# A two-layer fp32 encoder on one core: TensorE's order taken from the program text, attention steps spread over three pump steps, and a lane of their own for the gates

## The chip, the cores and the metric

The kernel runs on one core of a Trainium2 chip. The metric is device time in microseconds (us), from one launch to its end; lower is better. The engines are TensorE (PE in the profile; its weight loads are listed apart as PEld), VectorE (DVE), ScalarE (ACT), GpSimd (POOL) and SyncE (SP, which issues most DMAs). A profiled execution also gives the span from its first to its last instruction.

## What is computed

Two layers of a bidirectional encoder on x of 256 tokens by 2048, all in fp32. Cut to what matters:

```python
for l in range(2):
    h = rms_norm(x, gpre_mix)
    p = h @ W_in                       # 2048 x 4624: attention q,k,v; mLSTM q,k,v,o; 16 gate columns
    A = window_attention(rope(q), rope(k), v, sink)      # 8 heads of 128, 2 KV heads
    M = mlstm(forward + backward, chunks of 128)         # 4 heads, qk 128, v 256
    x = x + rms_norm(concat(A, M) @ W_out, gpost_mix)    # 2048 x 2048
    u = relu(rms_norm(x, gpre_mlp) @ W_up) ** 2          # 2048 x 8192
    x = x + rms_norm(u @ W_down, gpost_mlp)              # 8192 x 2048
```

Nothing fits a single reduced-precision product, so every weight and every activation is split into a rounded part and a remainder, and each product is made of three matmuls.

## The kernel before, in words

**Tiles.** Tokens are two tiles of 128, called t = 0 and 1; a contraction of 2048 is 16 chunks of 128, called k. Each weight tile covers 512 output columns (in the input projection, tile 3 has 272 and tile 9 has 256). Per layer there are 10 "in" tiles, 4 "out" tiles, and four blocks b of 4 "up" and 4 "down" tiles.

**Weights.** `load` (L168) brings one weight tile in four pieces: a DMA into `raw` (two buffers), an ACT copy that rounds it to `whi` (L191), a DVE subtraction that leaves `wlo` (L192), both with four buffers. The first two pieces of the program come in four parts each.

**Products.** `mm_k` (L196) issues, for one k and one t, three matmuls of 512 columns: hi by hi (L203), hi by lo (L204), lo by hi (L205). An up tile other than the first of its layer goes through `mm_stationary` (L259) instead: there the weights stay in the array and 256 tokens stream, in two pairs, each of 2 x 16 x 3 matmuls of 256 columns (L272 to L274). One two-bank tile `mms` holds both pairs. After each pair `up_evac` (L846) runs a Relu on ACT (L848), a square, and a split.

**Activations.** `pre` (L327) makes four chunks of a transposed, scaled input: four PE transposes into `ptx` (L332), a DVE multiplication into `xg` (L336), and `split_T` (L323), which is an ACT copy (L324) and a subtraction (L325) on DVE or POOL. At the start of the program, stage q of tile 0 (four k's) first calls `pre` for t = 0, does its 12 matmuls for t = 0, then the same for t = 1. The first up tile of a layer ends in `up_first` (L837): Relu, Square, four transposes `ptu` (L843), a split, for each t.

**Side work.** Attention and mLSTM are written as generators that stand in two lists, `urgent` and `later`; `mm_tile` (L220) advances the first generator of a list by one step after each k, through `pump` (L210). `attend` (L369) yields after the scores of each token tile, three times (`SLACK`, L366) before its transposes, and once between the transposes `pp` (L411) and the products `po` (L417). `gates` (L425), a chain of scans, is called by `side_gates` from the list `urgent`.

**What sets the order.** All instructions stand in program text in one order, the order of emission. A scheduler then gives every engine its own order, by a timeline that it computes: an instruction may be moved ahead of others of its engine whose inputs it takes to come later. Before the change it does so for all engines. Once given, an engine's order is fixed: an engine works through its own list.

Of the kernel before, what the change touches and what calls it, by code (L numbers as in the profile page):

```python
# [86 lines left out]
def encoder_kernel(ctx, tc, x, wall, rope, conv_w, gate_bias, ml_g, sink, gpre, gpost, out):  # L87
# [117 lines left out]
        nc.tensor.matmul(dst, lhsT=xl, rhs=hi, start=False, stop=(k == KC - 1))  # L205


    urgent, later = [], []

    def pump():  # L210
        for lane in (urgent, later):
            while lane:
                try:
                    next(lane[0])
                    break
                except StopIteration:
                    lane.pop(0)
        return urgent or later

    def mm_tile(key, T, stages=(), after=None, at=None, half=False):  # L220

# [101 lines left out]
    def split_T(ps, hi, lo, eng=None):  # L323
        nc.scalar.activation(hi, ps, AF.Copy)  # L324
        (eng or nc.vector).tensor_tensor(out=lo, in0=ps, in1=hi.bitcast(F32), op=ALU.subtract)  # L325
# [40 lines left out]
    SLACK = 3  # L366
    ASC = float(HD) ** -0.5

    def attend(pair, qT, kT, vA, nsink, snk, attT):  # L369

        g = pair // 2
        q0 = 2 * (pair % 2)
        ptile = []
        for t in range(NT):
            sc = psax.tile([P, 2, SEQ], F32, tag="ax", name="sc")
            far = slice((1 - t) * P, (2 - t) * P)
            for j in range(2):
                nc.tensor.matmul(  # L378
                    sc[:, j], lhsT=qT[:, q0 + j, t * P:(t + 1) * P], rhs=kT[:, g], start=(j == 0), stop=False)

            nc.tensor.matmul(
                sc[:, :, far], lhsT=identr, rhs=dmask[:, 1 - t:2 - t].to_broadcast([P, 2, P]),
                start=False, stop=True)
            mx = small.tile([P, 2], F32, tag="mx", name="mx")
            nc.vector.tensor_reduce(out=mx, in_=sc, op=ALU.max, axis=AX.X)
            nm = small.tile([P, 2], F32, tag="nm", name="nm")
            nc.vector.scalar_tensor_tensor(
                out=nm, in0=mx, scalar=-ASC, in1=nsink[:, 2 * pair:2 * pair + 2], op0=ALU.mult, op1=ALU.min)
            es = small.tile([P, 2], F32, tag="es", name="es")
            nc.vector.tensor_tensor(out=es, in0=snk[:, 2 * pair:2 * pair + 2], in1=nm, op=ALU.add)  # L390
            nc.scalar.activation(es, es, AF.Exp)
            pr = f2k.tile([P, 2, SEQ], F32, tag="f2k", name="pr")
            rs = small.tile([P, 2], F32, tag="rs", name="rs")
            for j in range(2):
                nc.scalar.activation(
                    pr[:, j], sc[:, j], AF.Exp, bias=nm[:, j:j + 1], scale=ASC, accum_out=rs[:, j:j + 1])
            nc.vector.tensor_tensor(out=rs, in0=rs, in1=es, op=ALU.add)
            nc.vector.reciprocal(out=rs, in_=rs)
            for j in range(2):
                nc.vector.tensor_scalar(  # L400
                    out=pr[:, j], in0=pr[:, j], scalar1=rs[:, j:j + 1], scalar2=None, op0=ALU.mult)
            ptile.append(pr)
            yield
        for _ in range(SLACK):
            yield
        po = psax.tile([P, 2, SEQ], F32, tag="ax", name="po")
        for j in range(2):
            pp = psax.tile([P, 2, SEQ], F32, tag="ax", name="pp")
            for kb in range(2):
                for t in range(NT):  # L410
                    nc.tensor.transpose(  # L411
                        pp[:, kb, t * P:(t + 1) * P], ptile[t][:, j, kb * P:(kb + 1) * P], ident)
            pT = f2k.tile([P, 2, SEQ], F32, tag="f2k", name="pT")
            nc.scalar.activation(pT, pp, AF.Copy)
            yield
            for kb in range(2):
                nc.tensor.matmul(  # L417
                    po[:, j], lhsT=vA[:, kb, g * HD:(g + 1) * HD], rhs=pT[:, kb], start=(kb == 0), stop=(kb == 1))
        split_T(po, attT[:, 2 * pair:2 * pair + 2, 0, :], attT[:, 2 * pair:2 * pair + 2, 1, :])
# [2 lines left out]
    CF = 0.25 * float(HD) ** -0.5  # L422
    DIRS = ((0, 0, 1), (32, 1, 0))

    def gates(gp, cols):  # L425


        f = gp.rearrange("p c (d q h) -> p c d q h", d=2, q=2)
# [19 lines left out]
        for d in range(2):  # L448
# [2 lines left out]
            nc.vector.scalar_tensor_tensor(  # L451
                out=gpad[:, :, 1, c0:c0 + MH], in0=ac[:, :, d], scalar=-2.0, in1=z[:, :, d],
                op0=ALU.mult, op1=ALU.add)
        yield
        pr = psax.tile([P, 2, SEQ], F32, tag="ax", name="prow")
        for q in range(2):
            for c in range(NT):
# [38 lines left out]
        for r, r2 in ((rnm, rnm2), (rwi, rwi2)):  # L496
            nc.scalar.activation(r2[:NG], r, AF.Copy)
            nc.vector.tensor_tensor(out=r2[NG2:NG2 + NG], in0=r, in1=r2[:NG].bitcast(F32), op=ALU.subtract)
        yield
        yield  # L500
        yield
        pc = psax.tile([P, 6, NG], F32, tag="ax", name="pcol")
        for i, r in enumerate((re_, rwe, rb)):
            for c in range(NT):
                nc.tensor.transpose(pc[:, 2 * i + c], r[:, c * P:(c + 1) * P], ident[:NG, :NG])
        nc.vector.tensor_copy(cols, pc)

    def conv_silu(zp, cw, dst):

        y = f1k.tile([P, SEQ], F32, tag="f1k", name="cy")  # L510
        nc.scalar.activation(y, zp, AF.Copy, scale=cw[:, 1:2])
        nc.vector.scalar_tensor_tensor(
            out=y[:, 1:], in0=zp[:, :SEQ - 1], scalar=cw[:, 0:1], in1=y[:, 1:], op0=ALU.mult, op1=ALU.add)
        nc.vector.scalar_tensor_tensor(
            out=y[:, :SEQ - 1], in0=zp[:, 1:], scalar=cw[:, 2:3], in1=y[:, :SEQ - 1], op0=ALU.mult, op1=ALU.add)
        th = f1k.tile([P, SEQ], F32, tag="f1k", name="cth")
        nc.scalar.activation(th, y, AF.Tanh, scale=0.5)
        nc.vector.scalar_tensor_tensor(out=dst, in0=th, scalar=1.0, in1=y, op0=ALU.add, op1=ALU.mult)

    def qk_heads(ps, c0, heads, s, cw, qk):  # L520

        w = 2 * HD * len(heads)
        nat = []
        for t in range(NT):
            a = f2k.tile([P, 512], F32, tag="f2k", name="qkn")
            nc.scalar.activation(a[:, :w], ps[t][:, c0:c0 + w], AF.Copy, scale=s[t])
            nat.append(a)
            yield
        yield
        for i, h in enumerate(heads):  # L530
            pt = psax.tile([P, 2, SEQ], F32, tag="ax", name="ptqk")
            for j in range(2):
                for t in range(NT):
                    o = (2 * i + j) * HD
                    nc.tensor.transpose(pt[:, j, t * P:(t + 1) * P], nat[t][:, o:o + HD], ident)
            for j in range(2):
                conv_silu(pt[:, j], cw[:, j * MH + h], qk[:, h, j])
            yield

    def mlstm_head(h, qk, va, cols, hm, hr, name):  # L540


        st = psax.tile([P, SEQ], F32, tag="ax", name="st")
        for c in range(NT):
# [118 lines left out]
    for l in range(DEPTH):  # L663
        big = apool.tile([P, 4112], F32, tag="A", name="A_mix")
        va = big[:, :NT * MH * (DV + 1)].rearrange("p (c h e) -> p c h e", c=NT, h=MH)
        qk = big[:, 2064:4112].rearrange("p (h j t) -> p h j t", h=MH, j=2)
        hm = big[:, 2064:4112].rearrange("p (h c e) -> p h c e", h=MH, c=NT)
# [7 lines left out]
        sh = [lay.tile([P, 1], F32, tag=f"sh{t}", name="sh") for t in range(NT)]  # L675
        cols = lay.tile([P, 6, NG], F32, tag="cols", name="cols", bufs=1)
        hr = [None] * MH

        def scales():
            for t in range(NT):  # L680
                s1[t] = pre_scale(t, "s1")
                nc.vector.tensor_scalar(out=sh[t], in0=s1[t], scalar1=0.5, scalar2=None, op0=ALU.mult)
# [29 lines left out]
        def side_gates(ps):  # L712
            gp = small.tile([P, NT, 16], F32, tag="gp", name="gp", bufs=1)
            for t in range(NT):
                nc.vector.scalar_tensor_tensor(
                    out=gp[:, t], in0=ps[t][:, :16], scalar=s1[t], in1=gbias, op0=ALU.mult, op1=ALU.add)
            yield from qk_heads(ps, 16, [0], s1, cw, qk)
            yield from gates(gp, cols)

        def side_v(ps, c0, h0, nh):  # L720
            for t in range(NT):
                nc.scalar.activation(
                    va[:, t, h0:h0 + nh, :DV], ps[t][:, c0:c0 + nh * DV].rearrange("p (h e) -> p h e", h=nh),
                    AF.Copy, scale=s1[t])
            for h in range(h0, h0 + nh):
                later.append(mlstm_head(h, qk, va, cols, hm, hr, f"l{l}h{h}"))
            yield

        gated = []
# [25 lines left out]
        for grp in range(2):  # L755
            ps = in_tile(1 + grp)
            urgent.append(side_q(ps, grp))
        ps = in_tile(3)
        urgent.append(side_gates(ps))
        ps = in_tile(4)  # L760
        urgent.append(qk_heads(ps, 0, [1, 2], s1, cw, qk))
        ps = in_tile(5)
        urgent.append(qk_heads(ps, 0, [3], s1, cw, qk))
        urgent.append(side_v(ps, 256, 0, 1))
        g = [gload(2 * l, n) for n in range(3)]
        ps = in_tile(6)
# [192 lines left out]
```

## Time and profile before

| | |
|---|---|
| median of 3 runs | 2148.2 us (2144.47 to 2152.57) |
| the profiled execution | 2145.2 us |
| its span | 2143.4 us |
| PE busy | 2100.0 us, 98% of the span |
| DVE, ACT, POOL busy | 53%, 46%, 3% |
| mean granted clock of PE | 0.996 |
| DMA | 388.37 MB, mean 181 GB/s |
| the chain that ended last | PE 92%, DVE 2%, DMA 2%, ACT 2% |

A row of a timeline gives the start, the duration of one piece of work and, in brackets, the idle time of its engine just before it with what ended that. Matmuls overlap in the engine, so the listed duration of one (0.39 us for 512 columns) is longer than the distance between two starts (0.23 us); costs are therefore read from starts. A busy share of PE near one says little by itself for the same reason. The granted clock is 1.00 at the full 2.4 GHz and 0.5 at 1.2 GHz.

### The profile page before, as it was taken

To read this page: it belongs to the slowest core of one execution; us is meant where nothing else is said; L and a number is where in the kernel's file an instruction comes from. 1 tells how busy PE (TensorE), PEld (TensorE's weight loads), DVE (VectorE), ACT (ScalarE), POOL (GpSimd) and SP (SyncE) were. 2 spreads that over 40 slices of the span, in tenths; PEclk is the share of its full clock that TensorE was granted. 3 is DMA by queue.
4 is the path that set the end of the run, shared out by engine and by line. 5 is a ranking of instruction groups with operands and counts; after the bars stand their busy time and mean duration, and the time that the engine had idled before them with its cause. 6 is when DMAs were issued, how large, how long until landed. Compare 5 with 4: busy or idle time off the path is not lost.

```text
span 2143.4 us, 28980 instructions
## 1 busy us (share of the span) xinstructions
PE 2100.0 (98%) x12412; PEld 1855.3 (87%) x12412; DVE 1135.4 (53%) x1219; ACT 983.9 (46%) x1077; POOL 60.8 (3%) x68
## 2 busy tenths in 40 slices
PE   8999999999999999999999999999999999999998
PEld 6878887988998998898878788879889989989986
DVE  6656566544444444445567656464444444444454
ACT  5455545453443353345354555455445434533542
POOL 0000002000000000000020000030000000000000
PEclk9999999999999999999999999999999999999999
DMA  7434355555555455546444344545555555554553
GB/s 256 163 135 175 120 194 180 197 192 190 188 194 191 169 197 207 186 174 215 174 181 161 134 150 148 206 149 195 207 190 193 189 190 183 195 193 173 191 205 118
DMA packets 62209, 388.37 MB, mean 181 GB/s; under 512 B 9600, under 2 KB 10112, under 8 KB 17280
## 3 DMA queue, kind: packets, MB, share of 16 engines
q1 hardware_dynamic: 61936, 386.48, 51.4%
q8 instruction: 97, 1.59, 0.3%
q14 instruction: 32, 0.26, 0.0%
q10 hardware_dynamic: 144, 0.03, 0.0%
HBM read 384.39 MB, written 2.10 MB: 180 GB/s over the span
## 4 chain that ended last, share of the span: by engine, by line
PE 92%; DVE 2%; DMA 2%; ACT 2%; POOL 1%; issue 1%; SPq 1%; POOLq 0%; DVEq 0%; ACTq 0%
PE mm L205 19%; PE mm L204 19%; PE mm L203 19%; PE mms L272 10%; PE mms L274 10%; PE mms L273 10%; DMA raw<-wall 1%; PE sc L378 1%; PE pn L594 1%; DVE xs L792 1%; PE po L417 1%; DVE wlo L192 1%; POOL h2T L325 1%; ACT whi L191 0%; ACT uz L848 0%
## 5 line engine op out<-in xcount | busy, mean ns | idle before, releaser
L192 DVE TENSOR_TENSOR wlo<-raw,whi 128x2048 fp32r<-128x2048 f32 (+3 forms) x374 | 828.8, 2217 | 885.7 <-ACT whi L191 885.3
L191 ACT ACTIVATE whi<-raw 128x2048 fp32r<-128x2048 f32 (+3 forms) x374 | 693.9, 1855 | 922.7 <-PE mm L205 506.6
L272 PE MATMUL mms<-h2T,whi 128*128 128x256 f32 x1920 | 535.2, 279 | 7.0 <-ACT uz L848 6.8
L273 PE MATMUL mms<-h2T,whi 128*128 128x256 f32 x1920 | 533.3, 278 | 0.0
L274 PE MATMUL mms<-h2T,wlo 128*128 128x256 f32 x1920 | 530.5, 278 | 0.0
L204 PE MATMUL mm<-wlo,uT 128*128 128x512 f32 x1024 | 398.5, 389 | 0.0
L203 PE MATMUL mm<-whi,uT 128*128 128x512 f32 x1024 | 398.5, 389 | 0.0
L205 PE MATMUL mm<-whi,uT 128*128 128x512 f32 x1024 | 398.2, 389 | 0.0
L272 PEld LDWEIGHTS mms<-h2T,whi 128*128 128x128 f32 x1920 | 360.7, 188 | 11.8 <-ACT uz L848 11.1
L273 PEld LDWEIGHTS mms<-h2T,whi 128*128 128x128 f32 x1920 | 362.3, 189 | 0.3
L274 PEld LDWEIGHTS mms<-h2T,wlo 128*128 128x128 f32 x1920 | 360.0, 188 | 0.0
L203 PE MATMUL mm<-whi,hT 128*128 128x512 f32 (+2 forms) x640 | 241.9, 378 | 8.8 <-ACT hT L324 6.4
L205 PE MATMUL mm<-whi,hT 128*128 128x512 f32 (+2 forms) x640 | 241.7, 378 | 1.4 <-POOL hT L325 1.4
L204 PE MATMUL mm<-wlo,hT 128*128 128x512 f32 (+2 forms) x640 | 241.0, 377 | 0.0
L204 PEld LDWEIGHTS mm<-wlo,uT 128*128 128x128 f32 x1024 | 192.2, 188 | 39.7
L203 PEld LDWEIGHTS mm<-whi,uT 128*128 128x128 f32 x1024 | 192.2, 188 | 39.7
L205 PEld LDWEIGHTS mm<-whi,uT 128*128 128x128 f32 x1024 | 192.2, 188 | 39.4
L203 PEld LDWEIGHTS mm<-whi,hT 128*128 128x128 f32 x640 | 121.8, 190 | 29.0 <-ACT hT L324 7.0
L205 PEld LDWEIGHTS mm<-whi,hT 128*128 128x128 f32 x640 | 121.6, 190 | 22.7 <-POOL hT L325 2.2
L204 PEld LDWEIGHTS mm<-wlo,hT 128*128 128x128 f32 x640 | 121.7, 190 | 19.8
L869 DVE SCALAR_TENSOR_TENSOR A_mlp<-mm,s2q,A_mlp 128x512 f32<-128x512 f32 x48 | 34.0, 747 | 37.0 <-PE mm L205 37.0
L203 PE MATMUL mm<-whi,memT 128*128 128x512 f32 x128 | 50.5, 394 | 0.0
(221 smaller groups left out, 1460.5 us busy)
## 6 DMA issues: line engine op xcount, KB each, us to landing
raw<-wall SPq DMA_DIRECT2D x350, 1024.0 KB, 4.8
raw<-wall SPq DMA_DIRECT2D x8, 544.0 KB, 3.6
g<-gpost SPq DMA_DIRECT2D x16, 256.0 KB, 4.5
raw<-wall SPq DMA_DIRECT2D x8, 512.0 KB, 3.5
xs<-x_in SPq DMA_DIRECT2D x8, 256.0 KB, 5.2
raw<-wall SPq DMA_DIRECT2D x8, 256.0 KB, 6.1
y_out<-xs SPq DMA_DIRECT2D x8, 256.0 KB, 2.8
cossin<-rope SPq DMA_DIRECT2D x1, 256.0 KB, 7.1
```

The source lines that it names most:

```text
L191: nc.scalar.activation(hi[:, sl], raw[:, sl], AF.Copy)
L192: nc.vector.tensor_tensor(out=lo[:, sl], in0=raw[:, sl], in1=hi[:, sl].bitcast(F32), op=ALU.subtract)
L203: nc.tensor.matmul(dst, lhsT=xh, rhs=hi, start=(k == 0), stop=False)
L204: nc.tensor.matmul(dst, lhsT=xh, rhs=lo, start=False, stop=False)
L205: nc.tensor.matmul(dst, lhsT=xl, rhs=hi, start=False, stop=(k == KC - 1))
L272: nc.tensor.matmul(ps[:, i], lhsT=hi[:, k], rhs=Tk[:, 0], start=(k == 0), stop=False)
L273: nc.tensor.matmul(ps[:, i], lhsT=hi[:, k], rhs=Tk[:, 1], start=False, stop=False)
L274: nc.tensor.matmul(ps[:, i], lhsT=lo[:, k], rhs=Tk[:, 0], start=False, stop=(k == KC - 1))
L325: (eng or nc.vector).tensor_tensor(out=lo, in0=ps, in1=hi.bitcast(F32), op=ALU.subtract)
L378: nc.tensor.matmul(sc[:, j], lhsT=qT[:, q0 + j, t * P:(t + 1) * P], rhs=kT[:, g], start=(j == 0), stop=False)
L417: nc.tensor.matmul(po[:, j], lhsT=vA[:, kb, g * HD:(g + 1) * HD], rhs=pT[:, kb], start=(kb == 0), stop=(kb == 1))
L869: nc.vector.scalar_tensor_tensor(out=acc[:, t, sl], in0=ps, scalar=s2[t], in1=acc[:, t, sl], op0=ALU.mult, op1=ALU.add)
```

## The change

Three edits. PE's order is no longer the scheduler's: it is the order of emission, while all other engines are still scheduled. `attend` yields three times where it yielded once, between `pp` and `po`. `gates` gets a lane of its own between `urgent` and `later`, yields 6 and 12 times where it yielded 1 and 3 times, and sets a flag that the mLSTM heads wait for before their first step.

```diff
-    urgent, later = [], []
+    urgent, scans, later = [], [], []
     def pump():
-        for lane in (urgent, later):
+        for lane in (urgent, scans, later):
...
-        return urgent or later
+        return urgent or scans or later
...
             nc.scalar.activation(pT, pp, AF.Copy)
-            yield
+            for _ in range(SLACK):
+                yield
             for kb in range(2):
...
-    def gates(gp, cols):
+    def gates(gp, cols, done):
...
-        yield
+        for _ in range(2 * SLACK):
+            yield
         pr = psax.tile([P, 2, SEQ], F32, tag="ax", name="prow")
...
-        yield
-        yield
-        yield
+        for _ in range(4 * SLACK):
+            yield
         pc = psax.tile([P, 6, NG], F32, tag="ax", name="pcol")
...
         nc.vector.tensor_copy(cols, pc)
+        done.append(True)
...
-    def mlstm_head(h, qk, va, cols, hm, hr, name):
+    def mlstm_head(h, qk, va, cols, hm, hr, name, ready):
+        while not ready:
+            yield
...
-            yield from gates(gp, cols)
+            scans.append(gates(gp, cols, gated_cols))
...
     with tile.TileContext(nc, schedule_with_timeline_sim=True) as tc:
-        encoder_kernel(tc, *args)
+        with tc.manual_schedule(engines={mybir.EngineType.PE}):
+            encoder_kernel(tc, *args)
```

How the orders moved is shown at three places. A number behind an underscore tells one buffer from another; "x4" is four alike in a row. Line numbers of the changed kernel are one higher from L208 on in the matmul code, and some six higher in the later parts.

PE at the start of the program. Before (two stretches):

```order
L332 MATMUL ptx<-ident,xs 128x128 x4
L203 MATMUL mm<-whi,hT_140 128x512
L204 MATMUL mm<-wlo,hT_140 128x512
L332 MATMUL ptx<-ident,xs 128x128 x4
L205 MATMUL mm<-whi,hT_140 128x512
...
L205 MATMUL mm<-whi,hT_140 128x512
L332 MATMUL ptx<-ident,xs 128x128 x12
L203 MATMUL mm<-whi,hT_140 128x512
```

Changed:

```order
L333 MATMUL ptx<-ident,xs 128x128 x4
L203 MATMUL mm<-whi,hT_142 128x512
L204 MATMUL mm<-wlo,hT_142 128x512
L205 MATMUL mm<-whi,hT_142 128x512
...
L205 MATMUL mm<-whi,hT_142 128x512
L333 MATMUL ptx<-ident,xs 128x128 x4
L203 MATMUL mm<-whi,hT_142 128x512
```

The eight groups of four transposes stood well ahead of the matmuls that use their chunks, twelve of them together. Now each group stands between the 12 matmuls of the group before and its own 12, and the same eight-fold pattern fills tile 0.

DVE in the same stretch, at stage q = 2. The `xg` and `hT` rows belong to `pre`; `wlo_201` and `wlo_203` are the first remainder of the tile after tile 0, in the two programs. Before:

```order
L336 TENSOR_TENSOR xg_314<-ptx_309,gcol_94 128x512
L336 TENSOR_TENSOR xg_335<-ptx_330,gcol_94 128x512
...
L192 TENSOR_TENSOR wlo_178<-raw_174,whi_177 128x2048
...
L325 TENSOR_TENSOR hT1_141<-xg_377,hT1_141 128x4x128
L682 TENSOR_SCALAR sh_197<-r_s11_434 128x1
L192 TENSOR_TENSOR wlo_201<-raw_199,whi_200 128x2048
```

Changed:

```order
L192 TENSOR_TENSOR wlo_203<-raw_201,whi_202 128x2048
L337 TENSOR_TENSOR xg_316<-ptx_311,gcol_96 128x512
L192 TENSOR_TENSOR wlo_209<-raw_207,whi_208 128x2048
L326 TENSOR_TENSOR hT1_143<-xg_316,hT1_143 128x4x128
L337 TENSOR_TENSOR xg_337<-ptx_332,gcol_96 128x512
L326 TENSOR_TENSOR hT1_143<-xg_337,hT1_143 128x4x128
L337 TENSOR_TENSOR xg_358<-ptx_353,gcol_96 128x512
L192 TENSOR_TENSOR wlo_215<-raw_213,whi_214 128x2048
```

Before, DVE had finished all eight groups of `pre` when the first remainder of the next tile came. Now three remainders of the next tile stand among the last four groups, two of them directly ahead of a row that PE waits for.

PE between the two pairs of one stationary up tile (the third of layer 0's up tiles; numbers tell one weight piece from another). Before:

```order
L274 MATMUL mms_3460<-h2T1_2881,wlo_3217 128x256
L272 MATMUL mms_3687<-h2T0_2880,whi_3437 128x256 [waits Activation_49]
L273 MATMUL mms_3687<-h2T0_2880,whi_3437 128x256
...
L273 MATMUL mms_3687<-h2T1_2881,whi_3437 128x256
L272 MATMUL mms_3460<-h2T0_2880,whi_3222 128x256 [waits Activation_49]
```

Changed:

```order
L275 MATMUL mms_3462<-h2T1_2883,wlo_3219 128x256
L273 MATMUL mms_3462<-h2T0_2882,whi_3224 128x256 [waits Activation_49]
L274 MATMUL mms_3462<-h2T0_2882,whi_3224 128x256
```

The 41 matmuls of the next tile that stood between the pairs are gone from there. The pair's last matmul and the next pair's first, which waits for ACT, are now neighbours, and so they are in all 30 stationary tiles of the program.

## Rows read from the trace of the kernel before

**Rows 1.** The page: shares of the chain that ended last, by engine.

```profile
PE 92%; DVE 2%; DMA 2%; ACT 2%; POOL 1%; issue 1%; SPq 1%; POOLq 0%; DVEq 0%; ACTq 0%
```

**Rows 2.** Timeline of PE from 0 to 40 us (start, us, engine, line, work, [idle before]).

```profile
3.75 1.08 PE L332 MATMUL ptx<-ident,xs 128*128 128x128 f32 x4 [3.75 <-POOL rwe L144]
8.45 0.80 PE L203 MATMUL mm<-whi,hT 128*128 128x512 f32 x1 [3.62 <-ACT hT L324]
...
17.69 1.47 PE L332 MATMUL ptx<-ident,xs 128*128 128x128 f32 x12
...
29.65 0.39 PE L203 MATMUL mm<-whi,hT 128*128 128x512 f32 x1
29.88 0.39 PE L204 MATMUL mm<-wlo,hT 128*128 128x512 f32 x1
...
38.52 0.41 PE L694 MATMUL pk<-ident,ra 128*128 128x128 f32 x2 [1.91 <-DVE ra L363]
```

**Rows 3.** Timeline of DVE from 4 to 40 us.

```profile
4.87 0.69 DVE L336 TENSOR_TENSOR xg<-ptx,gcol 128x512 f32<-128x512 f32 x1 [3.12 <-PE ptx L332]
...
8.52 0.69 DVE L325 TENSOR_TENSOR hT<-xg,hT 128x512 fp32r<-128x512 f32 x1
...
27.88 2.29 DVE L192 TENSOR_TENSOR wlo<-raw,whi 128x2048 fp32r<-128x2048 f32 x1 [0.22 <-ACT whi L191]
...
34.77 2.29 DVE L192 TENSOR_TENSOR wlo<-raw,whi 128x2048 fp32r<-128x2048 f32 x1 [3.86 <-ACT whi L191]
```

**Rows 4.** Timeline of ACT from 5 to 40 us.

```profile
7.78 0.61 ACT L324 ACTIVATE hT<-xg 128x512 fp32r<-128x512 f32 x1
...
32.82 1.92 ACT L191 ACTIVATE whi<-raw 128x2048 fp32r<-128x2048 f32 x1 [4.46 <-DMA raw<-wall]
```

**Rows 5.** Waits of PE: engine, work, releaser; us in total, times, longest.

```profile
PE mms L272 <- ACT uz L848: 6.8, 15, 0.5
PE mm L203 <- ACT hT L324: 6.4, 2, 3.6
...
PE pp L411 <- DVE pr L400: 3.0, 4, 1.2
PE po L417 <- ACT pT L414: 2.8, 2, 2.1
PE mm L203 <- ACT h2T L324: 2.7, 2, 1.3
PE mm L203 <- ACT qkn L526: 2.4, 2, 1.4
PE pk L694 <- DVE ra L363: 1.9, 1, 1.9
PE mm L205 <- POOL h2T L325: 1.5, 3, 0.7
PE mm L205 <- POOL hT L325: 1.4, 2, 0.7
```

**Rows 6.** Timeline of PE at one pair boundary, 750.2 to 751.5 us.

```profile
750.23 0.28 PE L274 MATMUL mms<-h2T,wlo 128*128 128x256 f32 x1
750.35 0.28 PE L272 MATMUL mms<-h2T,whi 128*128 128x256 f32 x1
...
751.20 0.39 PE L272 MATMUL mms<-h2T,whi 128*128 128x256 f32 x1 [0.45 <-ACT uz L848]
751.42 0.28 PE L273 MATMUL mms<-h2T,whi 128*128 128x256 f32 x1
```

**Rows 7.** Timeline of ACT at the same boundary.

```profile
750.55 0.60 ACT L848 ACTIVATE uz<-mms 128x512 f32<-128x512 f32 x1 [0.61 <-PE mms L274]
```

**Rows 8.** Stretches: us, busy PE PEld DVE ACT POOL, granted clock, DMA share, GB/s.

```profile
133.60:137.10 3.50, 3.50 (x12) 2.87 (x10) 1.45 (x4) 0.91 (x2) 0.00 (x0) 0.51 0.55 180
140.40:144.00 3.60, 3.26 (x8) 2.59 (x9) 0.89 (x4) 0.28 (x1) 0.00 (x0) 0.53 0.00 0
365.00:380.00 15.00, 12.99 (x66) 10.13 (x65) 12.12 (x27) 9.72 (x19) 8.29 (x7) 1.00 0.32 115
```

More of the change, by code (lines that the diff above doesn't have):

```diff
@@ L677, in encoder_kernel @@
         hr = [None] * MH
+        gated_cols = []
         def scales():
@@ L725, in side_v @@
             for h in range(h0, h0 + nh):
-                later.append(mlstm_head(h, qk, va, cols, hm, hr, f"l{l}h{h}"))
+                later.append(mlstm_head(h, qk, va, cols, hm, hr, f"l{l}h{h}", gated_cols))
             yield
```

## The prediction, made before the changed kernel ran

> **What bounds the kernel now.** I read the page's chain of waits first: 92% of the chain that ended last is PE [rows 1], so the time is set by how closely PE's instructions follow each other. Busy shares don't tell that, so I went through PE's timeline by starts. Two matmuls of 512 columns start 0.23 us apart in the steady state [rows 2], two of 256 columns 0.12 us [rows 6]. PE loses time against that pace only at a few places, and the list of PE's waits names them [rows 5]: 15 waits for the Relu between pairs, 0.45 us each; attention (`pp`, `po`, and the products after it, 3.0 + 2.8 + 2.4 = 8.2 us); the norms between phases (6.4 less the start's 3.6, 2.7, 1.5 and 1.4, together 8.4 us); the key transposes after tile 0 (1.9 us). To attention belong two stretches with a granted clock of about a half [rows 8], 7.1 us that at full clock would have taken half of that: 3.5 us more, so attention loses 11.7. All other matmuls run at their pace and are in both programs, so the change is worth what it does to these waits and what new ones it makes. No engine but PE, and no queue, is near its limit.
>
> The change fixes PE's order to that of the text. A scheduler that could put other matmuls into a wait can't do so any more. The three edits to the generators put distance back, but only around attention and the gates. So I went through the changed order place by place and asked for every instruction that waits: what was issued last before it, and how long is the chain from there?
>
> **The start.** Tile 0 needs eight groups of four transposes. Before, PE runs them early, twelve in one go at 17.69 us [rows 2], and after 8.45 us PE hardly stops until tile 0 ends; tile 1 begins at about 38.7, behind `pk` [rows 2]. Now each group stands directly ahead of its 12 matmuls. The chain from a group's last transpose is: 0.46 us to the start of `xg` (it starts at 4.87, the last transpose at 4.41, three steps of 0.22 after 3.75), 0.69 for `xg`, 0.61 for the rounded part on ACT, 0.69 for the remainder on DVE [rows 2 to 4]. The first matmul comes 1.9 us after the last transpose, where it could come after 0.1, and the third is 0.3 later still: some 2.0 us for each of seven groups, **14 us at least**. Nothing else can run meanwhile.
>
> More comes from DVE's and ACT's order. At q = 1 one remainder of a weight piece (2.29 us, [rows 3]) is ahead of the split that PE waits for, and one (done at 30.2, since it started at 27.88) is ahead of the second group's `xg`. At q = 2 the first piece of the next tile is ahead: its rounding starts at 32.82 and takes 1.92 [rows 4], its remainder runs from 34.77 to 37.06 [rows 3], then comes the group's `xg`, then a second remainder of 2.29, then the split. At q = 3 a rounding and a remainder stand between (1.92 and 2.29), and the rotary products of tile 0. Walked with these durations, the groups' matmuls end at 13.6, 19.0, 26.3, 34.4, 43.3, 48.3, 55.6 and 61 us. I add 4 us for groups at half clock, as seen after the waits of attention [rows 8]; up to four could lose 2.7 us each (12 x 0.23). Tile 1 then starts at 65 in place of 38.7: **+26**, with bounds of +14 and +35.
>
> **Pairs of up tiles.** The cut of two pairs shows the price [rows 6, 7]: the first pair's last matmul starts at 750.23, ACT's Relu at 750.55 for 0.60 us, the second pair's first matmul at 751.20, its next at 751.42. From the last matmul to that next one are 1.19 us. In the text's order two steps of 0.12 lie there: 0.96 us lost. Before, two borrowed matmuls stood between, so 0.72 was lost, 15 times: 10.8. The other 15 of the 30 tiles had more borrowed matmuls between and lost nothing. Now all 30 lose 0.96: 28.8 in all, **+18**. The bounds: +14 if the start after the wait costs no more than elsewhere (30 x 0.85, less 11), +22 if ACT is busy with a rounding at some of them.
>
> **First up tile of each layer.** Its eight transposes `ptu` came behind 14 and more matmuls of the next tile; now they follow the tile directly. A Relu (0.60, [rows 7]) and a square of the same size must pass for t = 0, the Relu of t = 1 among them, then ACT's order has a rounding of 1.92 [rows 4] ahead of the second square: 4.2 us from the last matmul to the second group, against 1.1 in a full queue: about 3.4 us per layer, **+7**, bounds +3 (without the rounding) and +8.
>
> **Attention.** Three steps of 6 matmuls are 4.1 us at 0.23, and cover `pp` to `po`; that wait (2.8, [rows 5]) goes. But steps of the 272-wide tile are short, half of that, and there the softmax of the second pair and the transposed queries before it come too early: between scores and `pp` stand a rounding and a remainder of weights on ACT and DVE (1.92 + 2.29). I find 1.3 + 3.1 us there and 5.0 at the third pair, 9.4 a layer, 18.8 in all, against 11.7: **+7**. Bounds: -11.7 if all of it is covered, +14 with clock loss like before's in both layers.
>
> **Gates, heads, norms.** The scans get 6 and 12 steps, and no wait of before stands there; the heads' flag is set many steps before they would use it: 0. `pk` now comes some k's into the next tile; its 1.9 us lies in the start's difference. At the norms the chains are as long as before and PE's waits stay within some 2 us in sum: 0, with bounds of -8.4 and +4. The tail after the last matmul is the same.
>
> **Sum.** 26 + 18 + 7 + 7 = 58 us on the profiled execution's 2145.2 (its span is 2143.4, which is 3 below the median of 2148.2): **2203 us**.
>
> **A rule against it.** What the rows show is that the half clock came with waits of 2 us in attention [rows 5, 8], while the stretch at 365 to 380 us, with waits of 1.3 and 0.7, kept a clock of 1.00 [rows 8]. The Trainium skill, page "TensorE: Matmul & The Clock Gate", section "Why this matters for your kernels", says that matmuls should stay back to back and that an engine which waits between its bursts runs them at the lower clock. By that rule all groups of the start from the second on would run cold, and the waits of attention would be followed by cold stretches too: about 2216 in place of 2203. The trace agrees for the long waits and not for the short ones.
>
> **The rivals.**
> 1. *The start costs its bare chain.* If DVE's and ACT's orders hurt less than I walked, since PE's groups shift so that remainders fall into idle time, the start costs 14, and attention about -2 to +3: 2145.2 + 14 + 18 + 7 = 2184, or 2177. For it: DVE is idle for 3.86 us before 34.77 [rows 3]. Against: the remainders stand in front of needed rows. Chance 0.17.
> 2. *Cold PE.* Each wait of 2 us or more is followed by half clock: seven groups at the start, four of them not hidden behind weights, 4 x 2.7 = 11 in place of 4, and two stretches a layer in attention, 4 x 1.7: 2203 + 7 + 7 = 2217. For it: [rows 8]. Chance 0.14.
> 3. *Not slower.* The distance of three steps covers every dependent wait outside the start and the pairs: attention's 11.7, the norms' 8.4 and `pk`'s 1.9 go, 22 us. With +18 for the pairs this is 4 us faster, 2141, if the start and the first up tiles cost nothing, and even at a cost of 4. It decides at the start: the transposed groups would have to cost less than 4 us in all. Against it: no row offers PE other work there. Chance 0.06 for a result within 0.5% (10.7 us, about what a measurement of this kernel tells from no change), 0.03 for faster.
> 4. *It does little.* The scheduler's order might be nearly the text's. But the three places shown differ just where PE waits. It has its chance within the 0.06.
>
> **How the numbers follow.** My forecast's own case, 2190 to 2215, has 0.60, the rivals 0.17, 0.14, and 0.09 for not slower. The range takes in the first two: from 2170 (start +14, attention -5, pairs +14) to 2222 (start +35, or cold PE). Faster by over 0.5%: 0.03, within: 0.06, slower: 0.91.
>
> **What would show it.** In the changed profile: tile 0's matmuls in groups of 12 with waits for `hT` of 2 to 4 us between, tile 1 starting near 65; 30 waits for `uz` with some 0.7 us of idle each; a wait of 3 us at `ptu` once a layer; no wait of `po` for `pT`; waits of `pp` or `pq` of 3 to 5 us at the 272-wide tile; granted clock a half only around the start and attention. It is wrong if tile 1 starts before 50, if fewer than 25 `uz` waits appear, or if attention has no wait.

## The result, and the profile after

The changed kernel takes 2320.1 us (median, 2317.8 to 2328.0) against 2149.0 before: a ratio of 1.080, 95% interval 1.077 to 1.084. It is 171 us slower. I had forecast 2203 with a range up to 2222: right in sign, and wrong by a factor of three in size.

First the chain that ended last, as in [rows 1], of the changed kernel:

```profile
PE 88%; ACT 5%; DVE 4%; issue 1%; DMA 1%; POOL 1%; POOLq 0%; SPq 0%; DVEq 0%; ACTq 0%
```

PE's share fell by four points, and ACT and DVE took them. The waits of PE, as in [rows 5]:

```profile
PE mms L273 <- ACT uz L854: 71.1, 30, 2.4
PE ptx L333 <- DVE xs L798: 17.5, 4, 6.9
PE mm L203 <- ACT hT L325: 16.0, 8, 3.1
PE pp L412 <- DVE pr L401: 13.8, 4, 4.3
PE mm L203 <- DVE part_ro L309: 11.8, 2, 5.9
PE ptu L849 <- ACT ur L846: 6.7, 4, 1.7
...
PE cp L582 <- issue: 2.6, 1, 2.6
PE cp L582 <- ACT kw L573: 2.6, 1, 2.6
```

Thirty waits for `uz`, as forecast, but of 2.4 us where I had some 0.7. The transposes after the norms and the matmuls of the last out tile (`part_ro`) have waits of 5 to 7 us; I had forecast none there. The wait of `po` for `pT` is gone.

To place the whole difference I took, for every two successive starts on PE, the distance less the median distance of that kind of matmul (its pace), and summed it over stretches of the program (us):

| place | before | changed | more | forecast |
|---|---|---|---|---|
| start, until tile 1 | 9.6 | 35.7 | 26 | 26 |
| attention, both layers | 12.9 | 23.4 | 10 | 7 |
| mLSTM heads | 0.9 | 16.3 | 15 | 0 |
| last out and down tiles, transposes after the norms | 13.6 | 45.5 | 32 | 0 |
| `ptu` | 0 | 7.7 | 8 | 7 |
| up and down blocks (pairs) | 17.6 | 101.6 | 84 | 18 |
| sum | 54.6 | 230.2 | 176 | 58 |

The two spans, 2317.9 and 2143.4, differ by 174.5, so the places hold all of it, within 2 us. Half of it is in one row.

Now one pair boundary, as in [rows 6, 7]. ACT of the changed kernel, in a timeline:

```profile
452.27 1.91 ACT L191 ACTIVATE whi<-raw 128x2048 fp32r<-128x2048 f32 x1 [3.51 <-PE mms L274]
454.09 0.58 ACT L854 ACTIVATE uz<-mms 128x512 f32<-128x512 f32 x1
```

And its PE:

```profile
452.07 0.28 PE L275 MATMUL mms<-h2T,wlo 128*128 128x256 f32 x1
454.72 0.38 PE L273 MATMUL mms<-h2T,whi 128*128 128x256 f32 x1 [2.37 <-ACT uz L854]
454.94 0.28 PE L274 MATMUL mms<-h2T,whi 128*128 128x256 f32 x1
```

PE's last matmuls of a pair release two things: L274 was the last reader of the piece `whi`, whose buffer is now free for the next piece, and L275 ends the pair. The rounding of the next piece begins at 452.27, before the pair's last result is there; the Relu is behind it in ACT's list and starts 1.8 us later. From 452.07 to 454.94 are 2.87 us, where two steps of 0.114 would do: 2.64 us lost, thirty times, 79 us. The kernel before had such Relus too. This is its ACT one tile before the boundary of [rows 7]:

```profile
727.82 1.92 ACT L191 ACTIVATE whi<-raw 128x2048 fp32r<-128x2048 f32 x1 [3.74 <-PE mms L273]
729.64 0.58 ACT L848 ACTIVATE uz<-mms 128x512 f32<-128x512 f32 x1
```

There 41 matmuls borrowed from the next tile lay between the pairs (5 us), and PE did not wait. The boundary at which I had read the price was one of those where PE did wait, and there the rounding had been done earlier, between the square and the split of the previous pair:

```profile
747.50 1.92 ACT L191 ACTIVATE whi<-raw 128x2048 fp32r<-128x2048 f32 x1 [0.48 <-DMA raw<-wall]
749.33 0.61 ACT L324 ACTIVATE uT<-uz 128x512 fp32r<-128x512 f32 x1
```

It is so throughout. Of the 60 Relus of the kernel before (one for each pair), 45 follow the end of a rounding on ACT by less than 0.1 us; at the 15 boundaries where PE waited, the Relu follows the split of `uz` 14 times, and once a rounding that had ended 0.26 us earlier. In the changed kernel all 60 follow a rounding.

The last out tile of layer 0 shows the same with both engines. ACT (first fence), DVE (second) and PE (third) of the changed kernel:

```profile
371.52 1.91 ACT L191 ACTIVATE whi<-raw 128x2048 fp32r<-128x2048 f32 x1 [3.52 <-PE mm L205]
373.34 0.58 ACT L314 ACTIVATE junk<-mm 128x512 bf16<-128x512 f32 x1
...
376.51 0.60 ACT L314 ACTIVATE junk<-mm 128x512 bf16<-128x512 f32 x1 [2.50 <-DVE part_ro L309]
```

```profile
373.47 2.29 DVE L192 TENSOR_TENSOR wlo<-raw,whi 128x2048 fp32r<-128x2048 f32 x1 [3.14 <-ACT whi L191]
375.68 0.15 DVE L308 TENSOR_REDUCE part_ro<-so 128x1 f32<-128x3 f32 x1
...
377.90 0.14 DVE L309 TENSOR_SCALAR part_ro<-part_ro 128x1 f32<-128x1 f32 x1
```

```profile
378.05 0.79 PE L203 MATMUL mm<-whi,attT 128*128 128x512 f32 x1 [5.88 <-DVE part_ro L309]
```

This tile begins with both token tiles in turn, so it needs both PSUM buffers, and the third tile's results must have left theirs. Their norms' partial sums stand behind a rounding of 1.91 and then behind a remainder of 2.29. In the kernel before, ACT (first line) and DVE had the same chain at the same place:

```profile
334.47 1.92 ACT L191 ACTIVATE whi<-raw 128x2048 fp32r<-128x2048 f32 x1 [3.52 <-PE mm L205]
336.42 2.29 DVE L192 TENSOR_TENSOR wlo<-raw,whi 128x2048 fp32r<-128x2048 f32 x1 [3.15 <-ACT whi L191]
338.63 0.15 DVE L307 TENSOR_REDUCE part_ro<-so 128x1 f32<-128x3 f32 x1
340.86 0.14 DVE L308 TENSOR_SCALAR part_ro<-part_ro 128x1 f32<-128x1 f32 x1
```

From the rounding's start to the end of the last `part_ro` are 6.5 us in both. But before, PE ran the last tile's 48 matmuls of t = 0 first, which need one buffer and take 10.9 us. The waits of 2.4 us and more that I followed back have such a rounding or remainder in them, but for the first of the program, which is for the input.

Last, half clock. Stretches of the changed kernel (us, busy of PE, PEld, DVE, ACT, POOL, granted clock): the first just after that wait, the second just after a pair's wait, the third a whole tile with its wait of 2.37 us.

```profile
378.00:382.50 4.50, 4.46 (x11) 3.53 (x12) 0.05 (x1) 0.00 (x0) 0.00 (x0) 0.51 0.57 226
641.50:645.50 4.00, 4.00 (x23) 4.00 (x23) 1.18 (x2) 0.07 (x1) 0.00 (x0) 0.57 0.60 193
466.00:490.00 24.00, 21.63 (x190) 21.43 (x190) 10.38 (x6) 11.00 (x10) 0.00 (x0) 1.00 0.48 173
```

By the starts, some 82 us of the changed kernel run at half the pace, in about 25 stretches, against 6 us before; 10 of the 30 waits between pairs are followed by one. Half of 82, 41 us, is lost by it, and this is in the table's places.

### The profile page after: what moved, and what is told of

It is laid out like the page before. It is cut to its first block, busy times and chain, and to the rows that moved or that the text cites. A ratio compares the mean times of both kernels' runs of the same rounds, so it can differ in the third digit from the quotient of the medians.

```text
span 2317.9 us, 28972 instructions
## 1 busy us (share of the span) xinstructions
PE 2152.0 (93%) x12412; PEld 1894.2 (82%) x12412; DVE 1137.8 (49%) x1219; ACT 983.6 (42%) x1077; POOL 58.6 (3%) x68
## 4 chain that ended last, share of the span: by engine, by line
PE 88%; ACT 5%; DVE 4%; issue 1%; DMA 1%; POOL 1%; POOLq 0%; SPq 0%; DVEq 0%; ACTq 0%
PE mm L203 18%; PE mm L205 18%; PE mm L204 18%; PE mms L273 10%; PE mms L274 10%; PE mms L275 10%; ACT whi L191 3%; DVE wlo L192 2%; DMA raw<-wall 1%; ACT uz L854 1%; PE pn L599 1%; POOL h2T L326 1%; DVE xs L798 0%; PE po L419 0%; PE ptx L333 0%
## 5 line engine op out<-in xcount | busy, mean ns | idle before, releaser
L273 PE MATMUL mms<-h2T,whi 128*128 128x256 f32 x1920 | 546.1, 284 | 71.1 <-ACT uz L854 71.1
L275 PE MATMUL mms<-h2T,wlo 128*128 128x256 f32 x1920 | 542.2, 282 | 0.0
L274 PE MATMUL mms<-h2T,whi 128*128 128x256 f32 x1920 | 542.1, 282 | 0.0
L273 PEld LDWEIGHTS mms<-h2T,whi 128*128 128x128 f32 x1920 | 371.3, 193 | 77.3 <-ACT uz L854 77.1
L274 PEld LDWEIGHTS mms<-h2T,whi 128*128 128x128 f32 x1920 | 371.4, 193 | 0.2
L275 PEld LDWEIGHTS mms<-h2T,wlo 128*128 128x128 f32 x1920 | 370.1, 193 | 0.0
L203 PE MATMUL mm<-whi,hT 128*128 128x512 f32 (+2 forms) x640 | 254.4, 398 | 17.0 <-ACT hT L325 16.0
L205 PE MATMUL mm<-whi,hT 128*128 128x512 f32 (+2 forms) x640 | 245.5, 384 | 4.1 <-DVE hT L326 4.1
L203 PEld LDWEIGHTS mm<-whi,hT 128*128 128x128 f32 x640 | 126.1, 197 | 39.3 <-ACT hT L325 18.3
L205 PEld LDWEIGHTS mm<-whi,hT 128*128 128x128 f32 x640 | 125.6, 196 | 30.3 <-DVE hT L326 7.8
L203 PE MATMUL mm<-whi,attT 128*128 128x512 f32 x128 | 52.6, 411 | 11.8 <-DVE part_ro L309 11.8
```

What stands on the lines that cost most here:

```text
L203: nc.tensor.matmul(dst, lhsT=xh, rhs=hi, start=(k == 0), stop=False)
L273: nc.tensor.matmul(ps[:, i], lhsT=hi[:, k], rhs=Tk[:, 0], start=(k == 0), stop=False)
L274: nc.tensor.matmul(ps[:, i], lhsT=hi[:, k], rhs=Tk[:, 1], start=False, stop=False)
L275: nc.tensor.matmul(ps[:, i], lhsT=lo[:, k], rhs=Tk[:, 0], start=False, stop=(k == KC - 1))
```

## The experiments

**e1_lanes: the generators' edits without the order.**

```diff
-        with tc.manual_schedule(engines={mybir.EngineType.PE}):
-            encoder_kernel(tc, *args)
+        encoder_kernel(tc, *args)
```

> The change without the fixed order of PE: the lane of the gates and the longer distances stay, PE is scheduled as before. Theory A (the loss is made by PE's order alone: what PE waits for stands in ACT's and DVE's lists behind the split of a weight piece): 2149 within 10 us, and some 15 waits for uz of 0.45 us. Rival C (the longer distances delay the gates and the heads, and that costs): over 2180.

Measured: 2133.1 us, a ratio of 0.994 (0.9925 to 0.9955). This part of the change alone makes the kernel faster. Its waits of PE begin so:

```profile
PE mms L273 <- ACT uz L854: 6.4, 14, 0.5
PE mm L203 <- ACT hT L325: 6.4, 2, 3.7
PE ptx L333 <- POOL rwe L144: 3.7, 1, 3.7
```

and have no row of `pp`, `po` or `qkn`, which [rows 5] had. The stretch with attention is full:

```profile
100.00:150.00 50.00, 50.00 (x248) 42.02 (x247) 37.51 (x94) 28.17 (x52) 0.00 (x0) 1.00 0.49 169
```

Before, attention lost 12.9 us above pace; the kernel got 12.8 faster (the kernel before took 2145.9 us beside it). Rival C is out, and the whole loss lies with PE's order. Theory A had expected no gain, so it missed that the scheduler can use the new distance.

**e2_order: the order without the generators' edits.**

```diff
+        with tc.manual_schedule(engines={mybir.EngineType.PE}):
+            encoder_kernel(tc, *args)
-        encoder_kernel(tc, *args)
```

> The fixed order of PE alone, the generators as in the kernel before. Theory A: 2320 to 2340, since only the attention steps get closer (some 2 us more for each pair at pp and po, 8 pairs), 30 waits for uz of 2.4 us. Rival C: near 2200, which was the forecast without any cost of the generators' edits.

Measured: 2329.0, a ratio of 1.085 (1.083 to 1.087), with the 30 waits for `uz` in full (71.1 us). The order of PE alone costs 183 us, and the changed kernel, which has the other edits too, is 9 us faster than this. The total is theory A's; where the difference between the two kernels lies is not. What the other edits take away is at the gates, whose transposed columns wait in this kernel and not in the changed one:

```profile
PE pcol L505 <- ACT rwe L493: 9.5, 4, 2.8
...
PE pcol L505 <- ACT rb L495: 3.6, 2, 1.8
```

At `pp` they don't help a fixed order: its waits are 5.3 us here and 13.8 in the changed kernel. Added up by place as in the table, attention, gates and heads together differ by about 1 us between the two profiled executions, which are 12 us apart. About 10 us lie at the pairs, where here 16 of the equal waits are followed by half clock and in the changed kernel 10. That the distances themselves help a fixed order is not shown.

**e3_pairbuf: a PSUM buffer for each pair.**

```diff
-        both = psmm.tile([P, 2, 512], F32, tag="mm", name="mms")
         for pair in range(2):
-            ps = both[:, pair].rearrange("p (i t) -> p i t", i=2)
+            ps = psmm.tile([P, 2, 512], F32, tag="mm", name="mms")[:, 0].rearrange("p (i t) -> p i t", i=2)
```

> The changed kernel with a PSUM buffer of its own for each of the two pairs of an up tile, so that the second pair waits for nothing of the first. Theory A: the 30 waits of 2.37 us go (2.64 each with the restart, 79 us) and with them the half clock behind some of them (10 stretches of 3.4 us at half, 17 us): 2320 - 96 = 2224, from 2215 to 2245, and no uz wait over 0.5 us. Rival D (the wait is only moved, to the weights of the next pieces, since DVE and ACT are behind): under 40 us gained, and PE waits for whi or wlo instead.

Measured: 2236.4, a ratio of 1.042 (1.040 to 1.044) to the kernel before. With the pairs' wait away 84 us go, the size of the table's last row; 12 less than expected, for which the last section has a reason. The two pairs had always written different halves of `both`; the wait came with the one buffer that they shared. No wait for `uz`, `whi` or `wlo` is in its list, so rival D is out.

**e4_dvewhi: the wait stays, the rounding ahead of the Relu goes.**

```diff
-                nc.scalar.activation(hi[:, sl], raw[:, sl], AF.Copy)
+                if stationary(order[i]):
+                    nc.vector.tensor_copy(hi[:, sl], raw[:, sl])
+                else:
+                    nc.scalar.activation(hi[:, sl], raw[:, sl], AF.Copy)
```

> The changed kernel with the rounding of the weights of stationary up tiles done by DVE, so that no rounding stands ahead of the Relu in ACT's list; the wait for uz stays. Theory A (the Relu stands behind a rounding of 1.92 us): the 30 waits shrink from 2.37 to about 0.7 us each, 50 us, and the half clock after them mostly goes, up to 17 us: 2253 to 2275. Rival B (the distance from the pair's end over the Relu to the next pair is that long by itself): waits of 2.4 us as before, 2320.

Measured: 2258.1, a ratio of 1.052 (1.051 to 1.054): 62 us less than the changed kernel. Its wait row is

```profile
PE mms L276 <- ACT uz L857: 34.3, 30, 2.4
```

Of the 30 waits 22 are of 0.69 to 0.75 us and 8 of 2.37. Those eight are the last up tile of each of the eight blocks, during which the weights of a down tile are loaded, and those are still rounded on ACT. This is ACT at two successive boundaries, the second of the eight kind:

```profile
468.81 0.60 ACT L857 ACTIVATE uz<-mms 128x512 f32<-128x512 f32 x1 [8.95 <-PE mms L278]
...
491.43 1.91 ACT L194 ACTIVATE whi<-raw 128x2048 fp32r<-128x2048 f32 x1 [3.52 <-PE mms L277]
493.25 0.58 ACT L857 ACTIVATE uz<-mms 128x512 f32<-128x512 f32 x1
```

This is the cleanest of the runs: one kernel holds both cases, the bare chain as I had priced it and the chain with a rounding ahead, and they differ by 1.7 us.

**e5_lanes_pairbuf: e1 and e3 together.**

```diff
-        with tc.manual_schedule(engines={mybir.EngineType.PE}):
-            encoder_kernel(tc, *args)
+        encoder_kernel(tc, *args)
...
+            ps = psmm.tile([P, 2, 512], F32, tag="mm", name="mms")[:, 0].rearrange("p (i t) -> p i t", i=2)
```

> PE scheduled as before, with the lanes and distances of the change and a buffer of its own for each pair. Theory A: the 14 waits for uz that are left there (6.4 us idle, 0.72 each with the two restarts, 10 us) go, and nothing else moves: 2133 - 10 = 2123, faster than both kernels. Rival (the scheduler's borrowed matmuls bring the same time, or the pieces come later): 2133.

Measured: 2133.0, a ratio of 0.9927 (0.9914 to 0.9940). No wait for `uz` is left, and it is no faster than e1_lanes. That is the rival's number, but not by its second reason: PE's waits for weights are no longer than in e1_lanes (0.8 us). The gain was given back in the pace of the matmuls; see the last section.

**e6_start: the start's transposes further ahead** (on top of e3_pairbuf).

```diff
-    for q in range(NPC):
-        in_stage[1][0, PK * q] = lambda q=q: pre(0, q, hT, 0, nc.vector)
-        in_stage[1][1, PK * q] = lambda q=q: pre(1, q, hT, 0, nc.vector)
+    ahead = [(0, 0), (0, 2), (1, 1), (0, 4), (1, 4), (0, 8), (1, 8), (0, 12)]
+    for i, at in enumerate(ahead):
+        in_stage[1][at] = lambda t=i % 2, q=i // 2: pre(t, q, hT, 0, nc.vector)
```

> The changed kernel with a buffer for each pair, and the transposes of the start written some 6 to 12 matmuls ahead of the matmuls that use them. Theory A: a wait of PE is what stands between in the text against what stands ahead in ACT's and DVE's lists, so 9 to 12 matmuls of 0.23 us (2.0 to 2.7) take off about 2 us at six or seven groups, and half clock goes with it: 2236 - 17 = 2219, from 2210 to 2228. Rival (the start is bound by weights and DVE): within 5 of 2236.

Measured: 2216.4, 20 us less than e3_pairbuf. The waits for `hT` from ACT fall from 17.2 us (8 of them) to 4.7 (3). The start was the chain against the distance.

**e7_norms: more distance at the phases' ends** (on top of e6_start).

```diff
-                mm_tile((l, "out", 0, n), mixT, [(PK, KC)], evac, pre_at(1, 10, 0, h2T, 2 * l + 1))
+                mm_tile((l, "out", 0, n), mixT, [(0, KC)], evac, pre_at(1, 10, 0, h2T, 2 * l + 1))
...
-                    mm_tile(key, h2T, [(0, KC - PK)], up_first, pre_at(0, 6, 1, h2T, 2 * l + 1))
+                    mm_tile(key, h2T, [(0, KC)], up_first, pre_at(0, 11, 1, h2T, 2 * l + 1))
...
-                    pt = psax.tile([P, 4, P], F32, tag="ax", name="ptu")
+                    def turn():
+                        for _ in range(8):
+                            yield
+                        pt = psax.tile([P, 4, P], F32, tag="ax", name="ptu")
...
+                    urgent.append(turn())
```

The last down tile and the first in tile of layer 1 are changed alike, and `mm_stationary` pumps after each k.

> The kernel e6_start with more matmuls in the text between dependents at the phases' ends as well: the last out and down tiles and the tile after each do all 16 k for one token tile first, the transposes of the second token tile come five k later, and ptu eight steps later. Theory A: at the last out tile 5.9 us of wait and 2 of half clock go in each layer (16), at ptx 4 us at three places (12), at ptu 3.6 in each layer (7): 2219 - 35 = 2184, from 2175 to 2198. Rival (the chains are longer than the distance and the waits only move): over 2205.

Measured: 2170.5, 46 us less than e6_start and more than I expected; a ratio of 1.010 (1.008 to 1.012) to the kernel before. The waits of `part_ro` and `ptu` are gone, those of `ptx` for `xs` fell from 17.5 to 6.8. With three places mended (the pairs' buffer, the start, the phases' ends), 150 of the 171 us are back, and PE's order is still that of the text. By place, the profiled execution still lies 12 us above the kernel before in attention, 11 in the heads and 6 at the start.

**e8_norms_sched: the text of e7_norms, PE scheduled.**

```diff
-        with tc.manual_schedule(engines={mybir.EngineType.PE}):
-            encoder_kernel(tc, *args)
+        encoder_kernel(tc, *args)
```

> The text of e7_norms with PE scheduled. Theory A: where the scheduler may move matmuls into a wait, the distance in the text is worth little: 2123 within 8 us, as for e5_lanes_pairbuf. Rival (the text's distance helps a scheduled order too): under 2113.

Measured: 2129.5, a ratio of 0.991 (0.990 to 0.992): the fastest kernel of this study, though only 4 us ahead of e1_lanes. Where the text's order was worth 150 us between two versions of the text, a scheduled PE hardly notices the difference.

**e9_banks: e5 with the second pair in the second bank.**

```diff
-            ps = psmm.tile([P, 2, 512], F32, tag="mm", name="mms")[:, 0].rearrange("p (i t) -> p i t", i=2)
+            ps = psmm.tile([P, 2, 512], F32, tag="mm", name="mms")[:, pair].rearrange("p (i t) -> p i t", i=2)
```

> As e5_lanes_pairbuf, but the second pair writes the second bank of its own buffer, as it did before, not the first. Open is why e5_lanes_pairbuf was no faster than e1_lanes though its waits were gone: its 256-column matmuls started 118 ns apart in most of the run, those of e1_lanes mostly 113 to 114. Theory P (the bank that is written sets the pace): the pace goes back to 113 to 114, and the time to 2133 - 16 = 2117. Theory Q (a stall sets the phase, and without stalls the slower pace stays): pace 118 and 2133 as before.

Measured: 2132.6, and nearly all matmuls of 256 columns at 118 ns. Theory P is out.

**e10_attend6: six steps between scores and `pp`** (on top of e7_norms).

```diff
             ptile.append(pr)
             yield
-        for _ in range(SLACK):
+        for _ in range(2 * SLACK):
             yield
```

> The kernel e7_norms (PE in the order of the text) with six steps in place of three between the scores and pp. Theory A: the four waits of pp (2.6 and 4.3 us in each layer) are chain against distance; three more steps of 6 matmuls are 2.2 us in the 272-wide tile and 4.1 us in the others, so most of 13.8 us goes, with the half clock after them: 2170 - 16 = 2154. Rival (DVE and ACT are ordered around PE's list, so that the softmax only comes later): within 5 of 2170.

Measured: 2160.1, 10 us less than e7_norms; two of the four waits of `pp` went, two stayed:

```profile
PE pp L412 <- DVE pr L401: 10.1, 2, 5.1
```

Half a hit. Two pairs got their distance; for the others the wait is now 5.1 us in place of 2.6 or 4.3, in the 272-wide tile. DVE and ACT are scheduled, so their lists can change with every edit of PE's; what stands ahead of `pr` here I did not follow. So distance in the text alone does not decide, and what stands ahead on the other engines must be looked up again after each edit.

**e11_break: an extra transpose ahead of each pair** (on top of e7_norms).

```diff
+            gap = psax.tile([P, 4, P], F32, tag="ax", name="gap")
+            nc.tensor.transpose(gap[:, 0], ident, ident)
```

> The kernel e7_norms with one extra transpose on PE, whose result nobody reads, ahead of every pair of the stationary up tiles (60 of them, some 0.11 us each, 7 us). Open is what sets the two paces of the 256-column matmuls, 113 to 114 and 118 ns. Theory Q1 (any other instruction between them sets the phase anew): a larger share at 113 to 114 than the 18% of e7_norms, and up to 20 us less: 2155 to 2170. Theory Q2 (only a wait of PE does): the share stays near 18%, and the time is 2170 + 7 = 2177.

Measured: 2171.0, as e7_norms; the share of the faster pace rose from 18 to 27%. It lies between the two theories and settles neither.

## Why the prediction was wrong

**The pairs of up tiles: mis-sized, +18 forecast, +84 found.** The step that failed is "Now all 30 lose 0.96: 28.8 in all". Count and place were right, and the bare chain was right too: e4_dvewhi shows 22 waits of 0.7 us, which is 0.96 to 1.02 with the restart. What the step left out is what stands ahead of the Relu in ACT's list; with it each boundary lost 2.64. The price came from a boundary where PE waited in the kernel before, and those were the cheap ones. At the hidden boundaries the Relu stood behind a rounding, and I never looked there since nothing waited. One such case lay open even before: the `po` wait of 2.1 us in [rows 5], whose copy of `pp` follows a rounding on ACT:

```profile
129.80 1.91 ACT L191 ACTIVATE whi<-raw 128x2048 fp32r<-128x2048 f32 x1 [1.90 <-PE mm L205]
131.62 0.58 ACT L414 ACTIVATE pT<-pp 128x512 f32<-128x512 f32 x1
```

I had named the case as a bound, "if ACT is busy with a rounding at some of them", and priced it at +22; it was all of them, because the matmuls that end the pair also free the buffer that the rounding waits for. On top came half clock after 10 of the 30 waits, some 16 us.

**Phase ends: 0 forecast, +32 found.** The step was "the chains are as long as before and PE's waits stay within some 2 us". The chain is as long, 6.5 us at the last out tile in both kernels; but before, matmuls could be moved into it. The last out tile's need for both PSUM buffers was in the text, and I had not priced it: 5.9 us a layer. At `xs` a remainder of 2.29 us stands ahead of the four residual rows:

```profile
409.38 2.29 DVE L192 TENSOR_TENSOR wlo<-raw,whi 128x2048 fp32r<-128x2048 f32 x1
411.58 2.73 DVE L798 SCALAR_TENSOR_TENSOR xs<-A_out,r_ro,xs 128x512 f32<-128x512 f32 x4
```

and PE's transposes begin at 412.48 after 5.15 us of idle time. e7_norms removed most of this by distance in the text.

**Heads: 0 forecast, +15 found.** "No wait of before stands there" was true and no reason. In layer 0 `cp` waits 2.6 us, with the end of `kw`, which had stood behind a rounding (start 215.04, the rounding ran from 212.92 to 214.83), and half clock follows. I tried no kernel that mends this place.

**The start, `ptu` and attention: right in size, and partly by luck.** The start cost 26 as forecast, and tile 1 began at 65.1, where I had said 65. There I had followed DVE's and ACT's lists row by row, and up to the seventh group the ends of my walk are within some 2 us of the measured ones. But half clock in four of the later groups cost 7 us and not 4, so the chains ended some 3 us earlier than I had walked them, and the two errors cancel. `ptu` cost 8 against 7, without some 4 us of half clock that came after it; in e4_dvewhi, where no rounding stands ahead of its squares, its waits fell from 6.7 to 2.5 us. Attention cost 10 against 7: its waits for `pq` and `pp` were 15.4 us where I had found 18.8, and half clock came on top. The three places where I went through the other engines' lists came out within 3 us each; the three where I priced the chain alone were 66, 32 and 15 off.

**The rivals.** The half clock of rival 2 came, and at more places than it named; its condition, that each wait of 2 us or more brings it, did not hold at 20 of the 30 pairs. The rule of the Trainium skill behind it (page "TensorE: Matmul & The Clock Gate", section "Why this matters for your kernels"), whose own example of an engine gone cold is one with a long wait before every matmul and which I had stretched to waits of 2 us, has the trace on its side at the long waits (0.51 after 5.88 us); at the pairs the same wait of 2.37 us was followed by a clock of 0.57 in one tile and by 1.00 through another. Rivals 1, 3 and 4 are out.

## What to carry to other kernels

If one engine's order is fixed by hand and the others stay scheduled, ask at every place where that engine waits what stands ahead of its releaser in the other engines' lists; here a rounding or a remainder of weights of about 2 us, freed by the same matmul, made a bare wait of 0.7 us into one of 2.4. Don't take a wait's price only from the places where it shows in the old trace: here, at the pairs, the scheduler had left the cheap ones exposed and hidden the dear ones, so look at a hidden one too. And test the parts of a change apart: here the generators' distance was worth 13 us with PE scheduled, and it was buried under 183 us from the edit next to it.

## What the runs showed that I had not expected

**Two paces of the same matmul.** The 256-column matmuls of the up tiles start either 113 to 114 ns or 118 ns apart, in long runs of one kind. Before, 60% of them are at the faster pace; in e1_lanes 65%, in e4_dvewhi 82%, in e5_lanes_pairbuf 18%, and in e9_banks 9%. With 5750 of them, the whole difference is 25 us. In e5_lanes_pairbuf the distances under 150 ns add up to 672 us, in e1_lanes to 656. Some 4 of these 16 us are the 36 such distances that e5_lanes_pairbuf has more; the other 12 are the pace, and they outweigh the 10 us of removed waits. The 12 us missing in e3_pairbuf are the same thing: the changed kernel has 65% at the faster pace, e3_pairbuf 19%. Here is the slower pace before (starts 0.12 apart), as in [rows 6], at a place without any wait:

```profile
749.76 0.28 PE L273 MATMUL mms<-h2T,whi 128*128 128x256 f32 x1
749.88 0.28 PE L274 MATMUL mms<-h2T,wlo 128*128 128x256 f32 x1
750.00 0.28 PE L272 MATMUL mms<-h2T,whi 128*128 128x256 f32 x1
```

The pace changes mostly where PE has waited or done something else. All kernels with waits between the pairs have 58 to 82% at the faster pace, all without them 9 to 27%. The bank written does not set it (e9_banks), and another instruction between raised the share a little (e11_break). What sets it stays open.

**Half clock after short waits.** Equal waits of 2.37 us, one in each up tile, were followed by half clock at some tiles and not at others: 10 of 30 in the changed kernel, 16 of 30 in e2_order, 4 of 8 in e4_dvewhi. Of the 22 waits of 0.7 us in e4_dvewhi none was. What decides between two equal waits no run here shows.
